# A decoder block's feed-forward part: four of seven products summed in one PSUM bank, memory pools laid anew at both layer changes, the last pair's norm moved into layer one

## The chip, the core and the metric

The kernel runs on one core of one Trainium2 chip. Its engines run side by side, each through its own instructions in a fixed order: PE (TensorE, matrix products), DVE (VectorE), ACT (ScalarE), POOL (GpSimd) and SP, which here issues nearly all DMAs. An engine waits for the others by semaphores, and nothing behind a waiting instruction runs before it. The metric is the time of one execution on the device in microseconds, as the median of several runs.

## The reference, cut to what matters

One decoder block over 2048 tokens of width 1024; the mixers in front are not touched by the change.

```python
h = h + jnp.einsum('bse,ed->bsd', mixed, w_out)
hn2 = rmsnorm(h, norm2_g)
up = jnp.einsum('bsd,df->bsf', hn2, w_up)        # 1024 -> 4096
act = jnp.square(jax.nn.relu(up))
h = h + jnp.einsum('bsf,fd->bsd', act, w_down)   # 4096 -> 1024
return rmsnorm(h, final_g)
```

## The kernel before

The tokens are handled in four tiles j of T = 512 columns, with the features on the 128 partitions. Every float32 operand is split into a high and a low part (`split`: ACT copies the high part, DVE subtracts it for the low one), and each 128x128 by 128x512 product is three matmuls.

**Output projection** (`tail`): for j = 0 to 3, eight chunks c, each of 24 matmuls into a bank `pd`. `add_acc` adds the result on DVE to the residual `acc`, and SP stores the sum to `hs[j][c]`. `norm2(j)` takes the root of the mean square (`pm` and `pr` are short matmuls on PE, the root itself runs on POOL) and multiplies `acc` by gain and root on DVE (L741).

**The two feed-forward layers** use a Strassen-Winograd scheme: the tiles are paired as (0, 1) and (3, 2), each matrix is halved both ways, and seven products of sums of quarters, P1 to P7, stand for eight. `PAIRS[0]` has its sums made by `sums_first`, which stores seven left operands to `su[0]`. For the second pair POOL stores the normed quarters to `su[1]` and `h21` (L745); `sums_second` loads them in layer one, in columns m = 4 to 7 of the first pair, makes four sums and stores them.

**Layer one** (`up`) runs over two pairs q, 16 columns m of the weights and the seven products s in a table `order`. One product is twelve matmuls (L907). `make_left` loads a left operand in two pieces into `sr` (two buffers) and splits them to `sa`; `make_weights` makes `hw` four products ahead; `make_left` runs `LA = 3` products ahead. Banks X, Y and Z have one buffer each: X holds P1 and then P2 on top, Y holds P6, P7 and P4 in a row, Z holds P5 and P3. After each product `post` takes from the banks what is complete so far: P1 is copied by ACT (L846), `u2`, `u3` and `a21` are made by DVE as Y plus that copy (L849, L855, L863), relu and square run on ACT (L840, L841), and results go to `sd` in DRAM (L837).

**Layer two** (`down`) loads 512 KB pieces of those results (`ar`, L965) and of the weights (`wr`, L929), splits them to `ad` and `wd`, and runs its seven products in steps of 48 matmuls (L1144) over the eight banks `pb`, two steps made ahead (`DA = 2`). The loads of the first two steps are on ACT's queue (`queue`), all later ones on SP's.

**What sets the order.** The program is written in order, and a scheduler then places each engine's instructions by its own estimate of times. Memory pools are laid out like a stack on two sides; a pool that takes the place of another waits for the last use of what lay there. `begin_ffn` opens layer one's pools at chunk c = 5 of the last tile's projection, prepares two left operands and the first weights, and the rest (`more`) is opened when the projection's pools are closed. The layer change in front of layer two lays `down`'s pools over those of `up`.

Of the kernel before, what the change touches and what calls it, by code (L numbers as in the profile page):

```python
# [15 lines left out]
P = 128  # L16
S = 2048
D = 1024
# [9 lines left out]
TB = T // P  # L28
WINDOWS = (2, 4, 8, 16)
# [4 lines left out]
RATIO_TAIL = 0.6  # L34
UA = 4
LA = 3
# [6 lines left out]
def hymba_block(ctx: ExitStack, tc: tile.TileContext, xT, gains, w_in, pool_w, w_out, w_up, w_down, out):  # L43
# [7 lines left out]
    wp = hp = pa = bigp = x0p = ntp = tmp = att = psd = psx = psz = pst = pso = olp = accp = acc2p = acc3p = None  # L51

    def open_pools(scope):
        nonlocal hp, wp, tmp, ntp, psd, psx, psz, pst, pso
        fpool = lambda name, bufs, **kw: scope.enter_context(tc.tile_pool(name=name, bufs=bufs, **kw))
        hp = fpool("hp", 2 * KD, side="right")
        ntp = fpool("ntp", 3, side="right")
        tmp = fpool("tmp", 2, side="right")
        wp = fpool("wp", 2, side="right")
        psz = fpool("psz", 2, space=PS)  # L60
        pso = fpool("pso", 1, space=PS)
        psd = fpool("psd", 2, space=PS)
        psx = fpool("psx", 1, space=PS)
        pst = fpool("pst", 2, space=PS)

    def open_big(scope):
        nonlocal bigp
        bigp = scope.enter_context(tc.tile_pool(name="bigp", bufs=1))
# [45 lines left out]
    zeros = const.tile([1, 1], I32, name="zeros")  # L114
    carry = const.tile([P, len(WINDOWS), PAD], F32, name="carry")
# [11 lines left out]
    h21 = [dram.tile([P, 2, T], F32, name=f"h21_{c}") for c in range(2)]  # L127
# [129 lines left out]
    def make_h():  # L257
        return hp.tile([P, 2, T], F32R, tag="h", name="h", align_bytes=256)
# [48 lines left out]
    def norm1_first():  # L307

        x, h = st[0]["x"], []
        for k in range(KD):  # L310
            d = make_h()
# [17 lines left out]
    def norm1(j):  # L329
        st[j]["h"] = normed(KD, lambda k: st[j]["x"][:, k], g1, make_h, lambda: st[j]["r"])  # L330
# [157 lines left out]
    def load_mix(j, n):  # L488
        st[j]["m"] = []
        for k in range(n):  # L490
            d = make_h()
# [8 lines left out]
    def tail(first):  # L500

        def root(j):

            if not (first and j < 2):
                drained(j)
                st[j]["todo"] = attn_norm(j, make_h)
# [18 lines left out]
        for j in range(NT):  # L525
# [3 lines left out]
            for c in range(KD):  # L529
# [10 lines left out]
                if c == 5 and j == NT - 1:  # L540
# [3 lines left out]

        def root_last():
            catch_up(len(later))
            norm2(NT - 1)
            catch_up(1)
        note(root_last)
# [174 lines left out]
    def square_of(j, key, c, first):  # L724
        if first:
            st[j][key] = tmp.tile([P, T], F32, tag="ss", name="ss", bufs=2)
# [9 lines left out]
    def norm2(j):  # L736
        acc = [st[j]["acc"][:, k] for k in range(KD)]
        later.append(lambda: st[j].update(rh=inv_rms(st[j]["sh"], D)))

        def put(k):  # L740
            nc.vector.scalar_tensor_tensor(acc[k], acc[k], g2[:, k:k + 1], st[j]["rh"], op0=ALU.mult, op1=ALU.mult)  # L741
# [34 lines left out]
    def up(pools, more):  # L776
# [3 lines left out]
        slots = [(q, m, s) for q in range(2) for m in range(NM) for s in range(7)]  # L780
# [17 lines left out]
        def make_weights(g):  # L798
            q, m, s = slots[g]
            which, i = order[s][1]  # L800
# [4 lines left out]
        def make_left(q, s):  # L805
            i, parts = order[s][0], []
            for c in range(2):
                r = srp.tile([P, 2, T], F32, tag="sr", name="sr")
                nc.sync.dma_start(r, su[q][i][c])
                t = saps[s].tile([P, 2, 2, T], F32R, tag="sa", name="sa", align_bytes=256)  # L810
# [4 lines left out]
        def sums_second(n):  # L815
            c, k = n // 2, n % 2
            new = lambda name: avp.tile([P, T], F32, tag="av", name=name)
            a11, a21, a12, s1 = new("ha11"), new("ha21"), new("ha12"), new("hs1")
            for t, of in ((a11, su[1][A11]), (a21, h21), (a12, su[1][A12]), (s1, su[1][A22])):
                nc.sync.dma_start(t, of[c][:, k])  # L820
            add = lambda to, x, y, op: nc.vector.tensor_tensor(to, x, y, op)
            add(s1, a21, s1, ALU.add)
            nc.sync.dma_start(su[1][S1][c][:, k], s1)
            add(a21, a11, a21, ALU.subtract)
            nc.sync.dma_start(su[1][S3][c][:, k], a21)
            add(a11, s1, a11, ALU.subtract)
            nc.sync.dma_start(su[1][S2][c][:, k], a11)
            add(a12, a12, a11, ALU.subtract)
            nc.sync.dma_start(su[1][S4][c][:, k], a12)

        def post(q, m, s):
# [12 lines left out]
            if s == 0:  # L844
                k["p1"] = pup.tile([P, T], F32, tag="p1", name="p1")
                nc.scalar.activation(k["p1"], x, AF.Copy)  # L846
            elif s == 1:
                k["u2"] = pup.tile([P, T], F32, tag="u2", name="u2")
                nc.vector.tensor_tensor(k["u2"], y, k["p1"], ALU.add)  # L849
            elif s == 2:  # L850
                act_of(A11, x, new("a11"))
                put(A11, k[A11])
            elif s == 3:
                k["u3"] = pup.tile([P, T], F32, tag="u3", name="u3")
                nc.vector.tensor_tensor(k["u3"], y, k["p1"], ALU.add)  # L855
            elif s == 4:
# [3 lines left out]
                put(A22, k[A22])  # L860
            elif s == 5:
                t = new("a21")
                nc.vector.tensor_tensor(t, y, k["p1"], ALU.add)  # L863
                act_of("A21", t, t)
# [8 lines left out]
            else:  # L873
# [10 lines left out]
        make_left(0, 0)  # L884
        add_weights(0, 0)
        for g in range(1, UA):
            make_weights(g)
        make_left(0, 1)
# [3 lines left out]
        for s in range(2, LA):  # L892
            make_left(0, s)
        for g, (q, m, s) in enumerate(slots):
            if g + LA < len(slots) and slots[g + LA][1] == 0:
                make_left(slots[g + LA][0], slots[g + LA][2])
            if q == 0 and s == 3 and 4 <= m < 8:
                sums_second(m - 4)
            bank, first = order[s][2:]
# [3 lines left out]
            last = (bank, s) in (("X", 2), ("Y", 5), ("Z", 6))  # L903
# [5 lines left out]
            post(q, m, s)  # L909
            if g + UA < len(slots):  # L910
                q2, m2, s2 = slots[g + UA]
                if s2 == 0:
                    add_weights(q2, m2)
                    n = q2 * NM + m2 + 1
                    if n < 2 * NM:
                        load(n // NM, n % NM)
                make_weights(g + UA)

    def down(pools):
# [18 lines left out]
        def make(g):  # L938
# [17 lines left out]
            else:  # L956
                w = blk(b22 if n == "P3" else b21, kk)
            t = t8.tile([P, 2, 2, T], F32R, tag="wd", name="wd", align_bytes=256)
            split((t[:, 0], t[:, 1]), w)
            if extra is not None:  # L960
                minus(blk(b12, kk), extra, 1, kk)
            left_ = {}
            for q in qs_:
                r = rs.tile([P, 2, T], F32, tag="ar", name="ar")
                queue[0].dma_start(r, sd[q][i][kk])  # L965
                left_[q] = s8.tile([P, 2, 2, T], F32R, tag="ad", name="ad", align_bytes=256)
                split((left_[q][:, 0], left_[q][:, 1]), r)
# [3 lines left out]
        ps = {}  # L971

# [347 lines left out]
```

## Time and profile before

| | before |
|---|---|
| median of 3 runs | 2015.91 us (2015.74 to 2019.39) |
| profiled execution | 2016.52 us, span 2014.6 us |
| mean granted TensorE clock | 0.983 |
| projection's last large matmul | starts at 722.85 us |
| layer one, second pair, undisturbed | 1100 to 1350 us |
| layer two's first matmul | starts at 1381.01 us |

Read the page's busy times first: PE is busy nearly all of the span. Such an engine is the bound, and what matters is where it falls behind its own pace; the other engines matter only where PE waits for them. For that one needs the table of stretches (busy time, count of instructions and granted clock in each), and then the timeline of the stretches that stand out. A busy PE can also be a slow PE, so the counts and the clock are read beside the busy time.

### The profile page before, as it was taken

To read this page: it belongs to the slowest core of one execution; us is meant where nothing else is said; L and a number is where in the kernel's file an instruction comes from. 1 tells how busy PE (TensorE), PEld (TensorE's weight loads), DVE (VectorE), ACT (ScalarE), POOL (GpSimd) and SP (SyncE) were. 2 spreads that over 40 slices of the span, in tenths; PEclk is the share of its full clock that TensorE was granted. 3 is DMA by queue.
4 is the path that set the end of the run, shared out by engine and by line. 5 is a ranking of instruction groups with operands and counts; after the bars stand their busy time and mean duration, and the time that the engine had idled before them with its cause. 6 is when DMAs were issued, how large, how long until landed. Compare 5 with 4: busy or idle time off the path is not lost.

```text
span 2014.6 us, 25952 instructions
## 1 busy us (share of the span) xinstructions
PE 1938.4 (96%) x9130; PEld 1613.1 (80%) x9130; DVE 1332.7 (66%) x1977; ACT 924.0 (46%) x1456; POOL 206.6 (10%) x415
## 2 busy tenths in 40 slices
PE   8999999999999979999999999996999999999997
PEld 6788788878888858878887888875888888888887
DVE  6877879667876976676687666654445453438474
ACT  5555556454644434545465455443232232333343
POOL 0212212102211120000000000000001000204010
PEclk9999999999999999999999999998999999999999
DMA  7675686788787874664565444457776654546472
GB/s 215 211 245 178 189 278 203 243 295 257 268 329 267 302 246 155 222 238 159 167 203 205 133 160 163 135 180 268 277 272 210 221 195 158 195 140 218 147 261 86
DMA packets 164396, 427.83 MB, mean 212 GB/s; under 512 B 19744, under 2 KB 25888, under 8 KB 160160
## 3 DMA queue, kind: packets, MB, share of 16 engines
q1 hardware_dynamic: 161824, 417.69, 61.9%
q10 hardware_dynamic: 1152, 4.19, 0.6%
q0 software_dynamic: 1280, 4.20, 0.6%
q8 instruction: 74, 1.21, 0.2%
q14 instruction: 66, 0.54, 0.1%
HBM read 284.44 MB, written 141.56 MB: 211 GB/s over the span
## 4 chain that ended last, share of the span: by engine, by line
PE 82%; DMA 7%; DVE 6%; issue 2%; ACT 1%; SPq 1%; POOL 0%; ACTq 0%; DVEq 0%; POOLq 0%
PE pb L1144 30%; PE pY L907 10%; PE pd L163 7%; PE pd L165 7%; PE pd L164 7%; PE pX L907 7%; PE pZ L907 7%; PE po L632 2%; DMA sr<-su 1%; PE pta L625 1%; DMA sd<-s 1%; DMA hs<-su 1%; DMA xt<-in_xT_dram 1%; PE pm L190 1%; PE pr L216 1%
## 5 line engine op out<-in xcount | busy, mean ns | idle before, releaser
L1144 PE MATMUL pb<-ad,wd 128*128 128x512 f32 x2640 | 603.1, 391 | 16.4 <-ACT ad L135 16.4
L1144 PEld LDWEIGHTS pb<-ad,wd 128*128 128x128 f32 x2640 | 496.3, 188 | 119.8 <-ACT ad L135 16.9
L163 PE MATMUL pd<-h,hl 128*128 128x512 f32 x768 | 309.6, 403 | 9.4 <-ACT h L312 6.3
L165 PE MATMUL pd<-h,hl 128*128 128x512 f32 x768 | 305.4, 398 | 0.9 <-DVE hl L136 0.9
L164 PE MATMUL pd<-h,hl 128*128 128x512 f32 x768 | 305.5, 398 | 0.3 <-DVE h L313 0.3
L907 PE MATMUL pY<-sa,hw 128*128 128x512 f32 x1152 | 281.2, 393 | 11.7 <-DVE sa L136 6.0
L907 PEld LDWEIGHTS pY<-sa,hw 128*128 128x128 f32 x1152 | 217.4, 189 | 59.9 <-DVE sa L136 7.1
L907 PE MATMUL pZ<-sa,hw 128*128 128x512 f32 x768 | 188.3, 393 | 8.0 <-DVE a L858 5.1
L907 PE MATMUL pX<-sa,hw 128*128 128x512 f32 x768 | 189.6, 390 | 1.9 <-ACT a L840 1.4
L135 ACT ACTIVATE ad<-ar 128x1024 fp32r<-128x1024 f32 x112 | 117.9, 1053 | 152.8 <-PE pb L1144 131.1
L136 DVE TENSOR_TENSOR ad<-ar,ad 128x1024 fp32r<-128x1024 f32 x112 | 141.9, 1268 | 65.5 <-ACT ad L135 65.5
L136 DVE TENSOR_TENSOR wd<-wr,wd 128x1024 fp32r<-128x1024 f32 x64 | 80.5, 1258 | 156.4 <-ACT wd L135 156.2
L163 PEld LDWEIGHTS pd<-h,hl 128*128 128x128 f32 x768 | 147.0, 191 | 38.8 <-ACT h L312 7.1
L907 PEld LDWEIGHTS pZ<-sa,hw 128*128 128x128 f32 x768 | 144.3, 189 | 41.3 <-ACT a L840 5.5
L165 PEld LDWEIGHTS pd<-h,hl 128*128 128x128 f32 x768 | 146.4, 191 | 30.3 <-DVE hl L136 1.4
L907 PEld LDWEIGHTS pX<-sa,hw 128*128 128x128 f32 x768 | 144.5, 188 | 32.6 <-ACT a L840 1.8
L164 PEld LDWEIGHTS pd<-h,hl 128*128 128x128 f32 x768 | 146.6, 191 | 28.7 <-DVE h L313 1.3
L135 ACT ACTIVATE wd<-wr 128x1024 fp32r<-128x1024 f32 x64 | 67.8, 1060 | 218.4 <-PE pb L1144 208.8
L135 ACT ACTIVATE hl<-raw 128x512 fp32r<-128x512 f32 x168 | 104.0, 629 | 124.5 <-PE pd L165 85.5
L136 DVE TENSOR_TENSOR hl<-raw,hl 128x512 fp32r<-128x512 f32 x168 | 114.8, 688 | 46.7 <-ACT hl L135 43.7
L135 ACT ACTIVATE hw<-rt 128x512 fp32r<-128x512 f32 x128 | 80.0, 626 | 91.3 <-PE pY L907 84.2
L840 ACT ACTIVATE a<-a 128x512 f32<-128x512 f32 x96 | 60.6, 632 | 128.7 <-DVE a L875 80.3
(186 smaller groups left out, 2343.0 us busy)
## 6 DMA issues: line engine op xcount, KB each, us to landing
ar<-sd SPq DMA_DIRECT2D x108, 512.0 KB, 4.4
wr<-in_w_down_dram SPq DMA_DIRECT2D x68, 512.0 KB, 3.8
rb<-in_w_up_dram SPq DMA_DIRECT2D x32, 1024.0 KB, 6.3
sd<-a SPq DMA_DIRECT2D x128, 256.0 KB, 4.6
raw<-in_w_in_dram SPq DMA_DIRECT2D x50, 512.0 KB, 4.3
sd<-s SPq DMA_DIRECT2D x96, 256.0 KB, 4.3
raw<-in_w_out_dram SPq DMA_DIRECT2D x32, 512.0 KB, 4.9
sr<-su SPq DMA_DIRECT2D x28, 512.0 KB, 4.1
```

The costliest lines, as they stand in the source:

```text
L135: nc.scalar.activation(hi, src, AF.Copy)
L136: return nc.vector.tensor_tensor(lo, src, hi.bitcast(F32), ALU.subtract)
L163: nc.tensor.matmul(ps, hl[:, 0, c], hi, start=(k == 0), stop=False)
L164: nc.tensor.matmul(ps, hl[:, 0, c], lo, start=False, stop=False)
L165: mm = nc.tensor.matmul(ps, hl[:, 1, c], hi, start=False, stop=(k == n - 1))
L190: marks["pm"] = nc.tensor.matmul(pm[:, c:c + 1], ss[:, c * P:(c + 1) * P], inv[n], start=(i == 0), stop=(i == len(parts) - 1))
L216: mm = nc.tensor.matmul(pr[:, b * P:(b + 1) * P], yr[:, x, b:b + 1].to_broadcast([P, P]), identr, start=(b == 0 and x == 0), stop=(b == TB ...
L625: nc.tensor.transpose(pt[:, x * P:(x + 1) * P], sg[:, x * P:(x + 1) * P], ident)
L632: nc.tensor.matmul(po[:, p * 256 + to:p * 256 + to + hi - lo], vw[:, 2 * p + v], at[:, x, lo:hi], start=(p == 0 and n == 0 and x == 0), sk ...
L840: nc.scalar.activation(t, src, AF.Relu)
L907: nc.tensor.matmul(t, w[:, wx, c], a[:, ax, c % 2], start=first and c == 0 and x == 0, stop=last and c == G - 1 and x == 2, skip_group_che ...
L1144: nc.tensor.matmul(ps[q, n], t[:, wx, c, n * P:(n + 1) * P], left_[q][:, ax, c], start=(kk == 0 and c == 0 and x == 0), stop=(kk == 7 and ...
```

## The change

- **Banks in layer one.** P1, P6, P7 and P4 all add up in Y, P2 alone is in X, P5 and P3 in Z. So P1, `u2` and `u3` are now plain copies of Y by ACT between the products, and DVE makes one sum with the copy of P1, for P2. X, Y, Z and a new R have two buffers each. The next column's P1 stands before this column's P4 and P3.
- **Layer two** sums P1, P6, P7 and P4 in one bank in the same way, and P5 with P3; the DVE sums between them become ACT copies or go.
- **The last pair's norm** goes out of the projection. `hs` in DRAM keeps the tiles before the norm; the root of tile 2 is kept in `rlast`, the root of tile 3 is made within layer one (behind its second and ninth product), and `sums_second` multiplies by gain and root when it loads a quarter, in columns 4, 6, 8 and 10, in three parts. It stores the quarters and the sums by SP; POOL's stores and `h21` go.
- **Left operands.** `begin_ffn` stands at c = 3 and prepares four left operands (`LB`); `sr` has four buffers (`SR`), and `LA` is 5.
- **Pools.** Half of the projection's operands lie on the left side, which `begin_ffn` frees; the DMA scratch area is smaller; `down`'s pools are laid in another order: `ar` (pool `rs`), `wr` (`rt`) and `wd` (`t8`) now lie on the pools of layer one's first weights, loads and left operands, where they lay in part on the tiles of its results (`avp`). All of layer two's loads are on SP's queue, with `ar` ahead of the split of the weights.

The core of the diff:

```diff
+SR = 4
+LB = 4
 UA = 4
-LA = 3
+LA = 5
...
-        hp = fpool("hp", 2 * KD, side="right")
+        hpb = fpool("hpb", KD, side="right")
...
+        hpa = scope.enter_context(tc.tile_pool(name="hpa", bufs=KD))
...
-                if c == 5 and j == NT - 1:
+                if c == 3 and j == NT - 1:
                     note(begin_ffn)
...
-        later.append(lambda: st[j].update(rh=inv_rms(st[j]["sh"], D)))
+        later.append(lambda: st[j].update(rh=inv_rms(st[j]["sh"], D, rlast[:, 0] if j == 2 else None)))
...
-            a = j == PAIRS[1][0]
-            if j in PAIRS[1]:
-                to = su[1][A12 if a else A22] if k >= 4 else su[1][A11] if a else h21
-                nc.gpsimd.dma_start(to[k % 4 // 2][:, k % 2], acc[k])
-        later.extend(lambda k=k: put(k) for k in range(KD))
+        if j in PAIRS[0]:
+            later.extend(lambda k=k: put(k) for k in range(KD))
...
-        order = ((A11, (0, 0), "X", True), (S2, (1, 1), "Y", True), (A12, (0, 1), "X", False), (S3, (1, 2), "Y", False),
-                 (S1, (1, 0), "Z", True), (A22, (1, 3), "Y", False), (S4, (0, 2), "Z", False))
+        what = {"P1": (A11, (0, 0), "Y", True, False), "P2": (A12, (0, 1), "X", True, True),
+                "P6": (S2, (1, 1), "Y", False, False), "P5": (S1, (1, 0), "Z", True, False),
+                "P7": (S3, (1, 2), "Y", False, False), "P4": (A22, (1, 3), "Y", False, True),
+                "P3": (S4, (0, 2), "Z", False, True)}
+        order = list(what)
+
+        slots = [cols[0] + ("P1",)]
+        for n, c in enumerate(cols):
+            slots += [c + (s,) for s in ("P2", "P6", "P5", "P7")]
+            slots += [c2 + ("P1",) for c2 in cols[n + 1:n + 2]]
+            slots += [c + (s,) for s in ("P4", "P3")]
...
+            def normed_of(h, i):
+                t, j = new("hn"), PAIRS[1][h]
+                nc.sync.dma_start(t, hs[j][i])
+                nc.vector.scalar_tensor_tensor(t, t, g2[:, i:i + 1], rlast[:, j - 2], op0=ALU.mult, op1=ALU.mult)
+                return t
...
+            def copy(name):
+                k[name] = pup.tile([P, T], F32, tag=name, name=name)
+                nc.scalar.activation(k[name], y, AF.Copy)
...
+            if g == 1:
+                y = inv_root(mean_squares([sslast], D, psu, "R"), nc.gpsimd)
...
+            elif g == 8:
+                pr = psu.tile([P, T], F32, tag="R", name="pr")
+                spread(pr, yrlast)
+                nc.scalar.activation(rlast[:, 1], pr, AF.Copy)
...
-        made, queue = {}, [nc.scalar]
+        made = {}
...
-            queue[0].dma_start(t, w_down[i, kk] if isinstance(i, int) else td[int(i[1]) - 1][kk])
+            nc.sync.dma_start(t, w_down[i, kk] if isinstance(i, int) else td[int(i[1]) - 1][kk])
...
-            if n_ == "P1":
-                nc.scalar.activation(val("p1", q)[:, n], b, AF.Copy)
-            elif n_ == "P6":
-                add(val("u2", q), val("p1", q))
-                add_residual(val("p1", q)[:, n], j0, 0, n)
-            elif n_ == "P7":
-                add(val("u3", q), val("u2", q))
-            elif n_ == "P4":
-                add(val("c21", q), val("u3", q))
-                add_residual(val("c21", q)[:, n], j1, 0, n)
+            if n_ in CHAIN:
+                nc.scalar.activation(val(CHAIN[n_], q)[:, n], b, AF.Copy)
+                if n_ in ("P1", "P4"):
+                    add_residual(val(CHAIN[n_], q)[:, n], j0 if n_ == "P1" else j1, 0, n)
...
-            rsp, tmp2, rlp = spool("rsp", 2), spool("tmp2", 2), spool("rlp", 2)
-            t8, rt, rs, s8 = spool("t8", DA + 1), spool("rt", 4), spool("rs", 3), spool("s8", 2 * DA + 1)
+            rlp, tmp2, rs, rt, t8 = spool("rlp", 2), spool("tmp2", 2), spool("rs", 3), spool("rt", 4), spool("t8", DA + 1)
+            s8, pup, rsp = spool("s8", 2 * DA + 1), spool("pup", 8), spool("rsp", 2)
```

How the order of the instructions moves is shown at three places. The first is DVE at the change from the projection to layer one, before: `acc_7414` is the last tile, `sa` are split left operands, `hw` weights.

```order
L136 TENSOR_TENSOR sa_8130<-sr_8128,sa_8130 128x1024
L136 TENSOR_TENSOR hw_8259<-rb_8083,hw_8259 128x512
L741 SCALAR_TENSOR_TENSOR acc_7414<-acc_7414,gains_130,r_8028 128x512 x8
L136 TENSOR_TENSOR sa_8153<-sr_8151,sa_8153 128x1024
L136 TENSOR_TENSOR hw_8282<-rt_8204,hw_8282 128x512
L136 TENSOR_TENSOR sa_8158<-sr_8156,sa_8158 128x1024
```

And of the change, where the last projection sum is followed by the sixth and fifth of the fresh operands (P4 and P7):

```order
L731 TENSOR_TENSOR acc_7418<-pd_7979,acc_7418 128x512
L142 TENSOR_TENSOR sa_8072<-sr_8070,sa_8072 128x1024
L142 TENSOR_TENSOR sa_8077<-sr_8075,sa_8077 128x1024
L180 TENSOR_TENSOR sslast_144<-sslast_144,sq_8006 128x512
L142 TENSOR_TENSOR hw_8120<-rb_8040,hw_8120 128x512
L142 TENSOR_TENSOR hw_8147<-rt_7800,hw_8147 128x512
L798 TENSOR_TENSOR rt_8187<-rb_8040 128x512
L800 TENSOR_TENSOR rt_8187<-rb_8040 128x512
L142 TENSOR_TENSOR sa_8044<-sr_8042,sa_8044 128x1024
```

The eight multiplications of the norm are gone from between the operands' splits. The second place is PE in an undisturbed column of layer one, before: the number behind a bank's letter is the column's buffer, so the rows show P5, P7, the next column's P1, P4 and P3.

```order
L907 MATMUL pZ_10228<-sa_8125,hw_10164 128x512 x6
L907 MATMUL pZ_10228<-sa_8130,hw_10164 128x512 x6
L907 MATMUL pY_10167<-sa_8097,hw_10146 128x512 x6
L907 MATMUL pY_10167<-sa_8102,hw_10146 128x512 x6
L907 MATMUL pX_10299<-sa_7865,hw_10225 128x512 x6
L907 MATMUL pX_10299<-sa_7870,hw_10225 128x512 x6
L907 MATMUL pY_10167<-sa_8153,hw_10182 128x512 x6
L907 MATMUL pY_10167<-sa_8158,hw_10182 128x512 x6
```

And of the change, from the next column's P1 over P7 and the next column's P2 to P4:

```order
L934 MATMUL pY_10259<-sa_7787,hw_10194 128x512 x4
L934 MATMUL pY_10109<-sa_8044,hw_10173 128x512 x6
L934 MATMUL pY_10109<-sa_8049,hw_10173 128x512 x6
L934 MATMUL pY_10259<-sa_7787,hw_10194 128x512 x2
L934 MATMUL pX_10326<-sa_7792,hw_10256 128x512 x6
L934 MATMUL pX_10326<-sa_7797,hw_10256 128x512 x6
L934 MATMUL pY_10109<-sa_8072,hw_10211 128x512 x6
L934 MATMUL pY_10109<-sa_8077,hw_10211 128x512 x6
```

Between P7 and P4, which share a bank and have a copy between them, stand fourteen matmuls of other banks. The third place is the change to layer two, before on ACT: relu and square of the last column (L840, L841), then the first loads and splits of layer two.

```order
L841 ACTIVATE a21_13016<-a21_13016 128x512
L840 ACTIVATE a12_13040<-a12_13040 128x512
L841 ACTIVATE a12_13040<-a12_13040 128x512
L965 DMA ar_13099<-sd0_0_0_308 128x1024
L965 DMA ar_13104<-sd1_0_0_364 128x1024
L965 DMA ar_13118<-sd0_0_1_309 128x1024
L135 ACTIVATE ad_13101<-ar_13099 128x1024
```

And of the change on SP, where `sd1_6_6` and `sd1_0_7` are stores of the last but one and of the last column:

```order
L993 DMA ar_13101<-sd0_0_0_312 128x1024
L993 DMA ar_13102<-sd1_0_0_368 128x1024
L993 DMA ar_13120<-sd0_0_1_313 128x1024
L864 DMA sd1_1_6_382<-a12_12785 128x512
L864 DMA sd1_6_6_422<-s4_12790 128x512
L864 DMA sd1_0_7_375<-a11_12809 128x512
L962 DMA wr_13099<-in_w_down_dram 128x1024
L962 DMA wr_13114<-in_w_down_dram 128x1024
```

The loads stood behind the last square of the last column on ACT and now stand ahead of the last column's stores on SP. On ACT of the change the first `ad` split stands behind three relus and three squares that follow the copy of P7, and the fourth load (`ar_13121`, the second pair's of the second step) is on SP behind most of the last stores. In the last column P7 and P4 follow each other on PE with nothing between them.

More of the change, by code (lines that the diff above doesn't have):

```diff
@@ L799, in make_weights @@
             q, m, s = slots[g]
-            which, i = order[s][1]
+            which, i = what[s][1]
+            if s == "P2":
+                add_weights(q, m)
             hl = hlp.tile([P, 2, G, P], F32R, tag="hw", name="hw", align_bytes=256)
@@ L805, in make_left @@
         def make_left(q, s):
-            i, parts = order[s][0], []
+            i, parts = what[s][0], []
             for c in range(2):
@@ L813, in make_left, with sums_second @@
             left_ops[q, s] = parts
[L815 removed]
+        SUMS, second = ("P2", "P5", "P4"), {}
+        def sums_second(n, part):
             c, k = n // 2, n % 2
             new = lambda name: avp.tile([P, T], F32, tag="av", name=name)
[L818 to L820 removed]
+            keep = lambda i, t: nc.sync.dma_start(su[1][i][c][:, k], t)
             add = lambda to, x, y, op: nc.vector.tensor_tensor(to, x, y, op)
[L822 to L829, printed above, removed]
+            def normed_of(h, i):
[3 more added lines that the diff above has]
+                return t
+            if part == 0:
+                second["a21"], a22 = normed_of(1, n), normed_of(1, 4 + n)
+                second["s1"] = new("hs1")
+                add(second["s1"], second["a21"], a22, ALU.add)
+                keep(A22, a22)
+                keep(S1, second["s1"])
+            elif part == 1:
+                a11, a21, s1 = normed_of(0, n), second["a21"], second["s1"]
+                add(a21, a11, a21, ALU.subtract)
+                second["s2"] = new("hs2")
+                add(second["s2"], s1, a11, ALU.subtract)
+                keep(A11, a11)
+                keep(S3, a21)
+                keep(S2, second["s2"])
+            else:
+                a12, s4 = normed_of(0, 4 + n), new("hs4")
+                keep(A12, a12)
+                add(s4, a12, second["s2"], ALU.subtract)
+                keep(S4, s4)
         def post(q, m, s):
@@ L842, in act_of @@
                 k[i] = t
[L844 to L856, printed above, removed]
+            def copy(name):
+                k[name] = pup.tile([P, T], F32, tag=name, name=name)
+                nc.scalar.activation(k[name], y, AF.Copy)
+            if s == "P1":
+                copy("p1")
+            elif s == "P2":
+                t = new("a11")
+                nc.vector.tensor_tensor(t, x, k["p1"], ALU.add)
+                act_of(A11, t, t)
+                put(A11, t)
+            elif s == "P6":
+                copy("u2")
+            elif s == "P7":
+                copy("u3")
                 t = new("a22")
@@ L883, in up @@
         make_weights(0)
-        make_left(0, 0)
-        add_weights(0, 0)
+        make_left(0, "P1")
+        make_left(0, "P2")
         for g in range(1, UA):
             make_weights(g)
-        make_left(0, 1)
+        for s in order[2:LB]:
+            make_left(0, s)
         yield
@@ L891, in up @@
         load(0, 1)
-        for s in range(2, LA):
-            make_left(0, s)
+        lefts = [(g, q, s) for g, (q, m, s) in enumerate(slots) if m == 0 and not (q == 0 and s in order[:LB])]
         for g, (q, m, s) in enumerate(slots):
[L895 to L899, printed above, removed]
+            while lefts and lefts[0][0] <= g + LA:
+                make_left(*lefts.pop(0)[1:])
+            if q == 0 and 4 <= m < 12 and m % 2 == 0 and s in SUMS:
+                sums_second(m // 2 - 2, SUMS.index(s))
+            bank, first, last = what[s][2:]
             if first:
```

95 lines of the change are left out of this document (46 added, 49 removed).

## The prediction

> **What bounds the kernel now.** First the page's busy times, then the table of stretches, to see where the bounding engine does not run at its pace.
>
> ```profile
> PE 1938.4 (96%) x9130; PEld 1613.1 (80%) x9130; DVE 1332.7 (66%) x1977; ACT 924.0 (46%) x1456; POOL 206.6 (10%) x415
> ```
>
> TensorE (PE) is busy 96% of the span. The change removes no large product, so it can only win what PE loses by standing still or by running at a lower clock. Where that is, the stretches tell (length, then busy time and count of each engine, granted clock, DMA share, GB/s):
>
> ```profile
> 1100.00:1350.00 250.00, 250.00 (x1105) 207.11 (x1104) 165.40 (x261) 125.13 (x209) 0.00 (x0) 1.00 0.45 150
> 720.00:760.00 40.00, 26.67 (x100) 19.80 (x99) 27.11 (x36) 17.86 (x24) 10.72 (x23) 0.83 0.67 231
> 840.00:910.00 70.00, 67.82 (x296) 55.00 (x295) 53.76 (x87) 33.73 (x58) 0.00 (x0) 1.00 0.71 244
> 1050.00:1090.00 40.00, 35.46 (x149) 26.93 (x148) 33.29 (x48) 25.32 (x38) 0.00 (x0) 1.00 0.65 228
> 1350.00:1400.00 50.00, 30.76 (x127) 24.52 (x126) 23.61 (x24) 16.82 (x20) 0.00 (x0) 0.83 0.83 282
> 1400.00:1900.00 500.00, 500.00 (x2207) 414.06 (x2206) 245.02 (x223) 153.98 (x163) 52.13 (x32) 1.00 0.61 205
> ```
>
> 1100 to 1350 is layer one undisturbed: 1105 matmuls in 250 us, 0.2262 us each, so a product of twelve takes 2.72 us. Four stretches fall behind that pace. The first holds 16 short matmuls of the norm beside the large ones:
>
> ```profile
> 728.52 0.95 PE L190 MATMUL pm<-inv,ss 128*128 128x1 f32 x8
> 737.27 1.27 PE L216 MATMUL pr<-identr,yr 128*128 128x128 f32 x8 [1.27 <-POOL yr L226]
> ```
>
> What each stretch loses, waits and slow clock together, is its length less its matmuls times 0.2262:
> - 720 to 760, the change from the output projection to layer one. Less the 16 short ones, some 2 us, it holds 84: 40 - 84 x 0.2262 - 2 = **19.0 us**.
> - 840 to 910, the columns in which the second pair's sums are made: 70 - 296 x 0.2262 = **3.0 us**.
> - 1050 to 1090, the change from the first pair to the second inside layer one: 40 - 149 x 0.2262 = **6.3 us**.
> - 1350 to 1400, the change to layer two: 50 - 127 x 0.2262 = **21.3 us**.
>
> Together 49.6 us. The other losses lie before 690 us, and there the two programs stand in the same order on every engine. Who ends PE's waits (total, times, longest):
>
> ```profile
> PE pb L1144 <- ACT ad L135: 16.4, 1, 16.4
> PE pY L907 <- DVE sa L136: 6.0, 2, 5.1
> PE pZ L907 <- DVE a L858: 5.1, 1, 5.1
> PE pZ L907 <- DVE a L875: 2.1, 3, 1.0
> ```
>
> **Change to layer two.** The timeline there (start, length, engine or queue, what; in brackets the idle time before it and who ended it):
>
> ```profile
> 1357.97 0.68 DVE L855 TENSOR_TENSOR u<-pY,p 128x512 f32<-128x512 f32 x1
> 1358.80 2.98 PE L907 MATMUL pY<-sa,hw 128*128 128x512 f32 x12 [2.81 <-DVE u L855]
> 1361.62 2.96 PE L907 MATMUL pZ<-sa,hw 128*128 128x512 f32 x12
> 1367.60 0.38 SPq L837 DMA_DIRECT2D sd<-s  x1
> 1373.36 5.11 ACTq L965 DMA_DIRECT2D ar<-sd  x3
> 1379.90 1.06 ACT L135 ACTIVATE ad<-ar 128x1024 fp32r<-128x1024 f32 x1 [8.99 <-DMA ar<-sd]
> 1380.99 1.23 DVE L136 TENSOR_TENSOR ad<-ar,ad 128x1024 fp32r<-128x1024 f32 x1 [9.35 <-ACT ad L135]
> 1381.01 19.37 PE L1144 MATMUL pb<-ad,wd 128*128 128x512 f32 x76 [16.43 <-ACT ad L135]
> ...
> 1367.60 5.73 DMA sd<-s
> 1373.36 6.44 DMA ar<-sd
> ```
>
> The last two lines are of the chain that ended last. The first `ar` load is issued at 1373.36, when a store of layer one's result (1367.60 + 5.73) has landed: the buffer of `ar` lies on memory of the tiles that are stored. The data is there 6.5 us later, and then comes a split. The relaid pools put `ar` and `wr` on memory that layer one has finished with, and the order has the three first `ar` loads ahead of the last column's stores. The loads of the first two steps also move from ScalarE's queue to SP's, where a row that waits holds up all behind it. With the memory free, the 16.43 us go. What is late next is worked out from the order. PE now runs P7 and P4 of the last column on one bank with nothing between them, and P4 waits for a ScalarE copy:
>
> ```profile
> L846 ACT ACTIVATE p<-pX 128x512 f32<-128x512 f32 x32 | 19.0, 594 | 6.3 <-PE pX L907 3.9
> L849 DVE TENSOR_TENSOR u<-pY,p 128x512 f32<-128x512 f32 x32 | 22.1, 690 | 22.9 <-PE pY L907 22.9
> L840 ACT ACTIVATE a<-a 128x512 f32<-128x512 f32 x96 | 60.6, 632 | 128.7 <-DVE a L875 80.3 <-DVE a L858 37.8 <-DVE a L863 8.4
> L841 ACT ACTIVATE a<-a 128x512 f32<-128x512 f32 x128 | 80.4, 629 | 3.1 <-ACT a L840 0.3
> ```
>
> That copy takes 0.59 us and its hand-overs some 0.2, my estimate: 0.8 us. From its end ScalarE has three relus and three squares and then the first `ad` split, 6 x 0.63 + 1.06 = 4.8 us, two of them behind VectorE sums of 0.69 us: 6.2 us, against 5.44 us of PE (P4 and P3). With hand-overs I take 1.5 us. The low half of that split stands behind four VectorE sums, of which PE covers some: 1.0 us. Sum **3.3 us**. The ends are 0 (ScalarE keeps up) and 8.8 us (a load and both halves of a split in full: 6.5 + 1.06 + 1.23).
>
> **Change to layer one.**
>
> ```profile
> 725.13 30.25 SPq L809 DMA_DIRECT2D sr<-su  x9
> 740.50 5.38 DVE L741 SCALAR_TENSOR_TENSOR acc<-acc,gains,r 128x512 f32<-128x512 f32 x8
> 745.80 1.22 DVE L136 TENSOR_TENSOR sa<-sr,sa 128x1024 fp32r<-128x1024 f32 x1
> 747.07 4.17 PE L907 MATMUL pY<-sa,hw 128*128 128x512 f32 x11 [5.05 <-DVE sa L136]
> 752.71 1.06 ACT L135 ACTIVATE sa<-sr 128x1024 fp32r<-128x1024 f32 x1 [8.28 <-DMA sr<-su]
> 756.38 3.33 PE L907 MATMUL pZ<-sa,hw 128*128 128x512 f32 x7 [5.13 <-DVE a L858]
> ...
> sr<-su SPq DMA_DIRECT2D x28, 512.0 KB, 4.1
> ```
>
> Here PE waits for left operands, each a pair of loads and splits. One of them stands behind the eight products of the last pair's norm (740.50, 5.38 us). The next ones wait for loads that only two `sr` buffers pass on: a load and its split take 4.1 + 1.06 + 1.23 = 6.4 us, where PE uses an operand up in 2.72. After the change the norm is gone from this place, four operands (10.9 us of PE) are ready instead of two (5.4), and four buffers keep two operands in flight. A fresh operand takes 4.1 + 2 x 1.06 + 1.23 = 7.5 us, which 10.9 covers and 5.4 did not. I leave **1.0 us** for hand-overs; the ends are 0 and one uncovered round of 6.4 us.
>
> The norm's sixteen products of that pair come back inside layer one, four of them and the four sums of before in every second of eight columns, with four loads and seven stores in place of four and four. VectorE is busy 53.76 of 70 us there now. It loses two sums per column to ScalarE, and Z gets a second bank, so the waits of `pZ` on L875 lose their cause: 3.0 us go, and 3.0 is also the upper end of what may stay.
>
> **Change of pairs.** The same two `sr` buffers hold this one up:
>
> ```profile
> 1065.70 6.24 SPq L809 DMA_DIRECT2D sr<-su  x2
> 1069.28 1.06 ACT L135 ACTIVATE sa<-sr 128x1024 fp32r<-128x1024 f32 x1 [3.43 <-DMA sr<-su]
> 1070.39 0.50 PE L907 MATMUL pY<-sa,hw 128*128 128x512 f32 x1 [1.58 <-ACT sa L135]
> ```
>
> With four, and operands asked for five products ahead instead of three (13.6 us against 8.2, where 7.5 are needed), I leave **0.5 us**; the ends are 0 and 6.3.
>
> **One bank for four products** costs nothing in the steady columns by my reading, and gains nothing, since PE is already busy 250 of 250 us. The tightest place is P7 to P4: fourteen matmuls lie between, 3.17 us, to cover 0.8. Two sums (L849, L855) become copies. In layer two (500 of 500 us busy) seven groups of six matmuls, 9.5 us, lie between a product and the next on its bank. Uncovered, a copy would cost 0.8 us a column, 51 us over 64 columns. The POOL DMAs that go were off PE's path.
>
> **The sum.** The profiled execution took 2016.5 us (span 2014.6 and 1.9 around it). 2016.5 - 49.6 = 1966.9 without these losses; + 3.3 + 1.0 + 0.5 = 1971.7, say **1972 us**. The median of the runs, 2015.9, is 0.6 lower.
>
> **A rule on the clock.** After the 16.43 us wait, 76 matmuls take 19.37 us, 0.253 from one start to the next, which is 2.0 us over the pace, and the granted clock of that stretch is 0.83; between 1050 and 1090 there are waits like the 1.58 us above, and the clock stays at 1.00. The Trainium skill, page "TensorE: Matmul & The Clock Gate", section "Part 1: The HAM clock gate (the "warmup" mystery)", puts the drop to half rate after one idle window of about 3.4 us; the trace agrees as far as it goes. By it none of the waits I leave would cost clock. The same page's section "A second HAM failure mode: psum-queue depth-cycling" speaks against this change: short idles between groups that cycle through banks would make the clock swing, and by it the waits that I leave would each bring slow matmuls. The stretch from 1050 to 1090 speaks against that.
>
> **The rivals.**
> - *Layer two's wait stays in part* (20%). The second pair's `ar` for the second step is still loaded behind the last stores. For it: a store took 5.7 us to land. Against: it is due only after 72 matmuls of layer two, 16.3 us. It gives 8.8 in place of 3.3, and 2.0 of slow clock: 1979.
> - *Layer one's early loads hold up the projection* (10%). They begin two products earlier, where the DMA engines were already full:
>
> ```profile
> 670.00:690.00 20.00, 20.00 (x90) 16.54 (x89) 18.00 (x25) 7.55 (x14) 0.00 (x0) 1.00 1.00 375
> ```
>
>   Four more loads of 0.52 MB at 375 GB/s are 5.6 us of transfer. If the weights wait for all of it: 1972 + 5.6 = 1978.
> - *Clock* (5%). The short waits bring a slow stretch at both layer changes, 2.0 us each: 1976.
> - *Slower than before* (3%). ScalarE comes late to the copies of the shared bank because relu, square and splits stand ahead of them in its order. The gain of 44 us is used up when each of 64 columns loses 0.7 us, that is, when P7's copy ends 3.9 us after P7 instead of 0.8; relu, square and one split ahead are only 1.9. At 0.8 us a column: 1972 + 51 = 2023.
> - *The change doesn't do what it says* (2%). The buffers still meet live memory, and the wait at layer two stays whole: 1972 - 3.3 + 21.3 = 1990.
>
> My forecast has 60%. The range reaches from 1966, all losses gone, to 1987, where the first three rivals meet (5.5 + 2.0 + 5.6 and 2.0 over the forecast). Faster by over 0.2% (about what a measurement of this kernel can tell from no change) 0.95, within it 0.02, slower 0.03.
>
> **What would show it.** Right: between 1300 and 1350 of the new span PE waits less than 5 us and the clock stays at 1.00; 40 us around the first `pY` hold about 170 matmuls; no `pZ` wait on a VectorE sum in the columns with the second pair's sums; `ar` loads issued before the last column's stores. Wrong: a repeated wait of `pY` on a ScalarE copy in each column, or `pd` waiting for `raw` loads.

## The result, and the profile after

The changed kernel takes 1969.59 us (median of 4 runs, 1966.36 to 1973.38) against 2016.11 us before; the ratio is 0.9766, with a 95% interval of 0.9745 to 0.9788. The profiled execution took 1970.99 us, 45.5 less than the profiled one of before; the forecast was 1972.

The page of after, its busy times, and then the table of stretches (length, busy time and count of each engine, granted clock, DMA share, GB/s):

```profile
PE 1929.2 (98%) x9130; PEld 1610.7 (82%) x9130; DVE 1268.3 (64%) x1881; ACT 958.7 (49%) x1544; POOL 191.9 (10%) x399
```
```profile
690.00:780.00 90.00, 90.00 (x411) 74.74 (x411) 62.94 (x93) 53.36 (x84) 13.72 (x30) 1.00 0.59 202
840.00:910.00 70.00, 70.00 (x310) 57.96 (x310) 53.24 (x86) 36.65 (x66) 0.00 (x0) 1.00 0.71 239
1000.00:1100.00 100.00, 98.08 (x426) 80.69 (x425) 71.75 (x105) 64.08 (x105) 0.00 (x0) 0.98 0.59 201
1300.00:1350.00 50.00, 48.66 (x212) 39.19 (x211) 32.71 (x43) 28.27 (x43) 0.00 (x0) 1.00 0.86 314
1300.00:1400.00 100.00, 98.66 (x433) 80.57 (x432) 58.18 (x64) 43.20 (x57) 0.00 (x0) 1.00 0.82 291
```

The same account as in the prediction, length less matmuls times 0.2262: the change to layer one, inside 690 to 780, loses nothing any more (TensorE busy 90 of 90); neither do the columns with the second pair's sums (70 of 70). The change of pairs, inside 1000 to 1100, still loses 100 - 426 x 0.2262 = 3.6 us, and the change to layer two, inside 1300 to 1400, 2.1 us. Of 49.6 us some 44 are gone. TensorE's waits between 650 and 1450 (total, times, longest) are two lines:

```profile
PE pY L934 <- ACT u L873: 2.6, 2, 1.9
PE pb L1171 <- DVE ad L142: 0.6, 1, 0.6
```

Both waits of the first line are for ScalarE's copy of the bank that is shared: one in the last column of the first pair, one in the last column of all. The timelines there, first of TensorE and ScalarE at the change of pairs, then of SyncE, TensorE and ScalarE at layer two (start, length, engine, what; in brackets the idle time before and who ended it):

```profile
1023.65 2.88 PE L934 MATMUL pX<-sa,hw 128*128 128x512 f32 x12
1028.45 4.45 PE L934 MATMUL pY<-sa,hw 128*128 128x512 f32 x12 [1.92 <-ACT u L873]
...
1020.59 0.62 ACT L868 ACTIVATE a<-a 128x512 f32<-128x512 f32 x1
1026.86 1.06 ACT L141 ACTIVATE sa<-sr 128x1024 fp32r<-128x1024 f32 x1 [5.64 <-DMA sr<-su]
1027.82 0.58 ACT L873 ACTIVATE u<-pY 128x512 f32<-128x512 f32 x1
```
```profile
1306.39 1.28 SPq L993 DMA_DIRECT2D ar<-sd  x3
...
1326.71 2.88 PE L934 MATMUL pY<-sa,hw 128*128 128x512 f32 x12
1330.28 3.01 PE L934 MATMUL pY<-sa,hw 128*128 128x512 f32 x12 [0.69 <-ACT u L873]
1333.13 2.88 PE L934 MATMUL pZ<-sa,hw 128*128 128x512 f32 x12
1336.03 2.20 PE L1171 MATMUL pb<-ad,wd 128*128 128x512 f32 x8
1338.86 21.38 PE L1171 MATMUL pb<-ad,wd 128*128 128x512 f32 x93 [0.64 <-DVE ad L142]
...
1329.63 0.60 ACT L873 ACTIVATE u<-pY 128x512 f32<-128x512 f32 x1 [2.04 <-PE pY L934]
1334.93 2.94 ACT L141 ACTIVATE ad<-ar 128x1024 fp32r<-128x1024 f32 x3
```

At the change of pairs P7 of the old column is through by 1023.65, and its copy would take 0.6 us. But in ScalarE's queue a split of the new pair's `sa` stands ahead of it, and that split waits 5.64 us for its `sr` load. So the copy comes at 1027.82, and P4, which adds to the same bank, starts 2.1 us late. At layer two the `ar` loads now go out at 1306.39, before the last column's stores, and the 16.43 us wait is gone. The signs that the prediction named hold: between 1300 and 1350 TensorE waits 1.3 us in all, the clock stays at 1.00, and no `pZ` wait is in the list.

### The profile page after: what moved, and what is told of

It reads as the page before. It is cut to its first block, busy times and chain, and to the rows that moved or that the text cites. A ratio compares the mean times of both kernels' runs of the same rounds, so it can differ in the third digit from the quotient of the medians.

```text
span 1969.2 us, 25982 instructions
## 1 busy us (share of the span) xinstructions
PE 1929.2 (98%) x9130; PEld 1610.7 (82%) x9130; DVE 1268.3 (64%) x1881; ACT 958.7 (49%) x1544; POOL 191.9 (10%) x399
## 4 chain that ended last, share of the span: by engine, by line
PE 91%; DMA 3%; DVE 3%; ACT 1%; issue 1%; SPq 0%; POOL 0%; DVEq 0%; ACTq 0%; POOLq 0%
PE pb L1171 30%; PE pY L934 17%; PE pZ L934 8%; PE pd L169 8%; PE pd L171 8%; PE pd L170 8%; PE pX L934 4%; PE po L632 2%; PE pta L625 1%; PE pr L222 1%; PE pm L196 1%; PE pz L567 1%; PE pz L568 1%; DMA xt<-in_xT_dram 1%; PE pb L1134 1%
## 5 line engine op out<-in xcount | busy, mean ns | idle before, releaser
L934 PE MATMUL pY<-sa,hw 128*128 128x512 f32 x1536 | 366.1, 390 | 2.6 <-ACT u L873 2.6
L934 PEld LDWEIGHTS pY<-sa,hw 128*128 128x128 f32 x1536 | 288.9, 188 | 63.6 <-ACT u L873 3.4
L142 DVE TENSOR_TENSOR hw<-rt,hw 128x512 fp32r<-128x512 f32 x128 | 87.6, 686 | 77.1 <-ACT hw L141 77.0
L873 ACT ACTIVATE u<-pY 128x512 f32<-128x512 f32 x64 | 38.1, 595 | 119.6 <-PE pY L934 119.5
L934 PE MATMUL pX<-sa,hw 128*128 128x512 f32 x384 | 92.7, 389 | 0.0
L966 DVE TENSOR_TENSOR wr<-wr 128x1024 f32<-128x1024 f32 x32 | 40.0, 1251 | 76.2 <-DMA wr<-in_w_down_dram 76.2
```

What stands on the lines that cost most here:

```text
L142: return nc.vector.tensor_tensor(lo, src, hi.bitcast(F32), ALU.subtract)
L873: nc.scalar.activation(k[name], y, AF.Copy)
L934: nc.tensor.matmul(t, w[:, wx, c], a[:, ax, c % 2], start=first and c == 0 and x == 0, stop=last and c == G - 1 and x == 2, skip_group_che ...
L966: nc.vector.tensor_tensor(b, a, b, ALU.subtract)
```

## The experiments

The runs of one group shared a chip and the runs of before beside them. Ratios are to before, with 95% intervals; the changed kernel's is 0.9766.

### The norm of the last pair put back (e1)

```diff
+            if j in PAIRS[1]:
+                to = su[1][A12 if a else A22] if k >= 4 else su[1][A11] if a else h21
+                nc.gpsimd.dma_start(to[k % 4 // 2][:, k % 2], acc[k])
+        later.extend(lambda k=k: put(k) for k in range(KD))
...
-            if q == 0 and 4 <= m < 12 and m % 2 == 0 and s in SUMS:
-                sums_second(m // 2 - 2, SUMS.index(s))
+            if q == 0 and s == "P7" and 4 <= m < 8:
+                sums_second(m - 4)
```

> The changed kernel with one part undone: the last pair's norm and its stores stand between the output projection and layer one again, and the sums of the second pair are made from the stored result in four columns. Theory (the eight products of the norm on VectorE and the root ahead of them, queued ahead of the splits of layer one's operands, were most of the 19.0 us that TensorE lost there): TensorE loses 10 to 16 us between 690 and 760, time 1980 to 1986. Rival (the loads through two buffers were most of it, and they are four now): at most 4 us lost there, time 1970 to 1974.

Measured: 1984.89 us, ratio 0.9835 [0.9811, 0.9860]. Its stretch, and who ends TensorE's longest waits:

```profile
690.00:780.00 90.00, 79.95 (x330) 64.03 (x330) 63.34 (x90) 42.77 (x66) 20.37 (x46) 0.92 0.67 236
```
```profile
PE pm L197 <- DVE sslast L181: 3.7, 1, 3.7
PE pd L170 <- DVE acc L738: 2.4, 1, 2.4
PE pY L925 <- ACT p L864: 2.0, 1, 2.0
```

81 matmuls fewer than in the changed kernel: 18.3 us, above what the theory expected, and almost as much as the 19.0 that stood there before, with four load buffers and four operands in place. So with the norm at this place the loss is there, and buffers alone don't cure it. But the way is not the one that the theory named: none of TensorE's waits here is for a left operand `sa`. The norm's short products `pm` wait 3.7 us for the last sum of squares, the projection waits 2.4 us for a sum that VectorE makes behind the other tile's eight multiplications, and 1.9 us go to weights `hw` (two shorter waits). The waits are 10.1 us in all (90 less 79.95); the rest is slow clock, 0.92 in this stretch. (The time rose by 15.3 and not 18.3; this kernel loses nothing at the change of pairs, where the changed one loses 3.6.)

### Two load buffers (e2, e11), and three products ahead (e12)

```diff
-SR = 4
+SR = 2
```

> The changed kernel with two buffers for the raw left operands of layer one in place of four. Theory (two buffers pass on one operand at a time, 6.4 us for each where TensorE uses one up in 2.72): a wait for sa splits comes back at the change of pairs, about 1 to 6 us, and 0 to 6 at the change to layer one; time 1972 to 1980. Rival (four operands made ahead and five asked ahead suffice by themselves): 1968 to 1971.

> The changed kernel with two load buffers, beside the changed kernel on one chip. Theory (two buffers hold the splits back in ScalarE's queue, so that fewer of them stand ahead of the copy): 2 to 4 us less than the changed kernel, no wait of TensorE at the change of pairs. Rival (the earlier run was lower by chance): within 1 us of it.

The third of them also has

```diff
-LA = 5
+LA = 3
```

> The changed kernel with two load buffers and operands asked three products ahead instead of five, as before the change, but with the four premade operands and the new order of the products. Theory (buffers and lead made the 6.3 us at the change of pairs): TensorE waits there for sa splits again, 2 to 6 us. Rival (the old order of the products and its two banks made them): under 1 us lost there.

Measured: e2 1967.33 us, ratio 0.9751 [0.9732, 0.9770]; the same kernel again, e11, 1968.63, 0.9761 [0.9741, 0.9781], beside the changed kernel (e9) with 1970.17, 0.9754 [0.9733, 0.9775]; e12 1966.97 (two runs). None is told from the changed kernel by its time. The stretch with the change of pairs, of e2, e11 and e12 in turn:

```profile
1000.00:1100.00 100.00, 100.00 (x443) 82.81 (x442) 72.70 (x106) 65.79 (x108) 0.00 (x0) 1.00 0.66 224
```
```profile
1000.00:1100.00 100.00, 98.10 (x430) 80.34 (x429) 71.77 (x104) 64.31 (x105) 0.00 (x0) 1.00 0.63 214
```
```profile
1000.00:1100.00 100.00, 100.00 (x443) 82.82 (x442) 76.60 (x113) 66.86 (x109) 0.00 (x0) 1.00 0.64 216
```

The theory of e2 and e12 fell: with two buffers, and even with two buffers and three products ahead, nothing is lost there in one execution each. In another execution of the two-buffer kernel (e11) 2.7 us were, with waits for `sa` splits of 1.0 and 0.9 us: it runs close to the edge. In time e11 lies 1.5 us under e9, between what its theory and its rival said, and the intervals overlap. With the rest of the change in place, then, neither the buffers nor the lead are needed to be rid of most of the 6.3 us. That the new order of products and banks took them away is not shown: it wasn't tried by itself, and the moved norm and the four premade operands were also in place.

### Two operands made ahead (e3)

```diff
-LB = 4
+LB = 2
...
-LA = 5
+LA = 3
...
+            sap[2], sap[3] = (spool(f"sap{s}", 2) for s in (2, 3))
```

> The changed kernel with two left operands made before layer one in place of four, asked three products ahead in place of five; four load buffers stay. Theory (two ready operands are 5.4 us of products, a fresh one takes 7.5 us): one uncovered round, 2 to 6 us at the change to layer one; time 1972 to 1976. Rival (with the norm gone from there and four buffers, nothing waits): 1968 to 1971.

Measured: 1979.42 us, ratio 0.9815 [0.9791, 0.9839].

```profile
690.00:780.00 90.00, 86.73 (x391) 71.12 (x390) 60.65 (x88) 50.59 (x80) 16.58 (x30) 1.00 0.54 191
...
1300.00:1400.00 100.00, 93.85 (x398) 76.26 (x397) 52.63 (x59) 40.63 (x55) 0.00 (x0) 0.95 0.76 266
```

At the change to layer one 20 matmuls are missing, 4.5 us, within the size that the theory expected. (The three products ahead alone don't do it: e12 has those, and is busy 89.5 of the 90 us.) But the round of fresh operands that the theory named is not what TensorE waits for. Its waits between 690 and 780 are these four:

```profile
PE pY L934 <- ACT u L873: 1.1, 1, 1.1
PE pr L222 <- POOL yrlast L939: 1.1, 1, 1.1
PE pr L222 <- POOL yr L232: 0.8, 1, 0.8
PE pr L222 <- POOL yrlast L940: 0.3, 1, 0.3
```

None is for an `sa`. One is for a copy of the shared bank, which starts on ScalarE directly behind an `sa` split; the other three are for the norm's roots, which POOL makes. So with the norm moved, two ready operands cost time here, but a fresh operand that takes 7.5 us is not shown to be why. The other large loss is at the change to layer two, 10.0 us. The two pools that are opened later also move layer two's buffers, and that these now meet live memory may be the reason, but it is not shown: the first `ar` load goes out at 1306.4 as in the changed kernel, and TensorE still waits 3.8 and 1.6 us for `ad`. The time, 3 us above what was expected, says nothing of the operands.

### The pools of before (e4), the queue of before (e5), both (e6)

```diff
-            sap[6], pup, rbb, avp = spool("sap6", 2), spool("pup", 2), spool("rbb", 1), spool("avp", 11)
+            avp, rbb, pup, sap[6] = spool("avp", 11), spool("rbb", 1), spool("pup", 2), spool("sap6", 2)
...
-            rlp, tmp2, rs, rt, t8 = spool("rlp", 2), spool("tmp2", 2), spool("rs", 3), spool("rt", 4), spool("t8", DA + 1)
+            rsp, tmp2, rlp = spool("rsp", 2), spool("tmp2", 2), spool("rlp", 2)
+            t8, rt, rs, s8 = spool("t8", DA + 1), spool("rt", 4), spool("rs", 3), spool("s8", 2 * DA + 1)
```

> The changed kernel with the pools of both layers laid in the order of before; loads on the sync engine's queue and ahead of the last stores as now. Theory (the buffers of ar on memory of tiles that layer one still stores set the wait at layer two): the first ar load is issued only after a store has landed, TensorE waits 9 to 17 us at its first pb products; time 1978 to 1988. Rival (the queue and the place of the loads in it set the wait, not the memory): under 3 us more than the changed kernel, 1969 to 1973.

```diff
-        made = {}
+        made, queue = {}, [nc.scalar]
...
-            rows = {q: rs.tile([P, 2, T], F32, tag="ar", name="ar") for q in qs_}
-            for q in qs_:
-                nc.sync.dma_start(rows[q], sd[q][i][kk])
...
+                r = rs.tile([P, 2, T], F32, tag="ar", name="ar")
+                queue[0].dma_start(r, sd[q][i][kk])
```

> The changed kernel with the loads of layer two's first two steps on ScalarE's queue and each ar load behind its step's weights, as before; the pools as now. Theory (the memory set 9 of the some 19 us between the two kernels at layer two; the queue and the place of the loads set the rest): the ar loads are issued later than 1306 and TensorE loses 5 to 12 us at the change, time 1973 to 1980. Rival (with free memory the queue does not matter): at most 3.5 us lost there, 1968 to 1972.

> The changed kernel with both the pools and the queue and load order of before; the banks and the order of the seven products stay. Theory (memory and queue together are the whole of it): TensorE loses 17 to 22 us at layer two, time 1984 to 1990. Rival (the old order of the products, its last sum on VectorE, had its own part in the wait): 10 to 14 us lost, 1977 to 1982.

Measured: e4 1979.15 us, 0.9810 [0.9781, 0.9840]; in the next group, where before took 2019.93, e5 1971.94, 0.9756 [0.9739, 0.9772], and e6 1982.10, 0.9796 [0.9774, 0.9819]. The stretch of layer two's change in e4, e5 and e6:

```profile
1300.00:1400.00 100.00, 91.77 (x389) 74.59 (x389) 50.30 (x56) 40.02 (x52) 0.00 (x0) 0.95 0.76 270
```
```profile
1300.00:1400.00 100.00, 97.88 (x431) 80.39 (x430) 56.78 (x63) 43.37 (x57) 0.00 (x0) 1.00 0.81 285
```
```profile
1300.00:1400.00 100.00, 90.39 (x382) 73.40 (x381) 52.81 (x59) 39.83 (x53) 0.00 (x0) 0.93 0.73 260
```

By the account above 12.0, 2.5 and 13.6 us are lost, against 2.1 in the changed kernel and 21.3 before, in one profiled execution each. By these, memory is worth 9.9 us (the interval of e4's time still touches that of the changed kernel, so the size rests on the stretch); the queue and the place of the loads are worth 0.4 when the memory is free, and 1.6 when it isn't. So the rival of e5 holds, and that of e6: 7.7 us of the old loss came from neither. What remains between e6 and before at this place is the rest of the change, the order of the products on the banks above all; it was not undone alone. In e4 the users of the tile `ar` show where the memory bites (what they waited for: total, times):

```profile
  DMA sd<-a: 4.8, 1
  DMA sd<-s: 4.6, 1
```

The first line is ScalarE's half of a split, the second VectorE's. Both wait for stores, not for the load, which went out at 1322.3, some 19 us before (the slowest `ar` load in this stretch took 7.8): so the buffers of the halves that they write, `ad`, lie on live memory as well. By this trace, freeing `ar` alone would not have been enough.

### P7 and P4 side by side in every column (e7)

```diff
+        slots = [c + (s,) for c in cols for s in ("P1", "P2", "P6", "P5", "P7", "P4", "P3")]
...
+                if s in ("P1", "P2") and fourth:
+                    behind.enter_context(tc.issue_after(fourth[0].ins))
```

> The changed kernel with the first product of the next column queued behind P4, so that P7 and P4 stand side by side on the shared bank in every column, as in the last one. Theory (the copy between them costs 0.85 us and the products between hide it): 0.85 us lost in each of 64 columns, 54 us, time 2022 to 2026. Rival (other products still stand between in the queue, or the copy is hidden another way): under 15 us more, below 1985.

Measured: 2019.96 us, ratio 0.9996 [0.9984, 1.0007]: the whole gain is gone. The waits between 690 and 1420, and one column's rows:

```profile
PE pY L934 <- ACT u L870: 35.5, 58, 1.8
```
```profile
1102.17 0.39 PE L934 MATMUL pZ<-sa,hw 128*128 128x512 f32 x1
1103.02 3.01 PE L934 MATMUL pY<-sa,hw 128*128 128x512 f32 x12 [0.46 <-ACT u L870]
1106.72 5.28 PE L934 MATMUL pY<-sa,hw 128*128 128x512 f32 x22 [0.69 <-ACT u L870]
```

The price of an uncovered copy is what the last column of the changed kernel showed (0.69 us of wait, and a start 0.85 us later than at the usual pace). The sum in the expectation came near for a wrong reason: there are 32 columns, not 64 (384 matmuls on `pX`, twelve a column), and in each two copies are uncovered, since a single matmul stands between P6 and P7 too: 46 us in 32 columns are 1.4 a column. Without the products between, then, the shared bank costs as much as the whole change gains.

### One bank for Z (e8)

```diff
-                ps[q, m, bank] = psu.tile([P, T], F32, tag=bank, name="p" + bank)
+                ps[q, m, bank] = psu.tile([P, T], F32, tag=bank, name="p" + bank, bufs=1 if bank == "Z" else 2)
```

> The changed kernel with one bank for Z in place of two. Theory (the second bank took the waits of pZ on VectorE's sums away): waits of pZ on a VectorE sum come back in the columns with the second pair's sums, 3 to 8 us in all, time 1972 to 1978. Rival (VectorE's lighter columns alone took them away): no such wait, 1968 to 1971.

Measured: 1972.03 us, ratio 0.9763 [0.9745, 0.9782], not told from the changed kernel. One wait of `pZ` on a VectorE sum is there between 690 and 1000, 0.5 us. The theory's 3 to 8 us are not: the second bank was not what took away most of these waits. (At layer two it loses 5.9 us in its one profiled execution, 416 matmuls between 1300 and 1400; why was not followed up.)

### The copy ahead of the split (e10), beside the changed kernel (e9)

```diff
-                make_left(*lefts.pop(0)[1:])
+                loaded.append(lefts.pop(0))
+                load_left(*loaded[-1][1:])
...
+            while loaded and loaded[0][0] <= g + LS:
+                with tc.issue_after(copied[0].ins):
+                    split_left(*loaded.pop(0)[1:])
```

> The changed kernel itself, as the measure for the three runs beside it on this chip. Both theories: the wait of pY on ScalarE's copy at the change of pairs, 1.9 us, and the slow matmuls behind it are there again; ratio to before 0.975 to 0.979.

> The changed kernel with layer one's raw left operands of the second pair loaded as now, but each one's splits on ScalarE queued behind the copy of the product before, so that the copy of P7 in the last column of the first pair no longer stands behind a split that waits for its load. Theory (the place in ScalarE's queue makes the wait): the 1.9 us wait and its slow matmuls go, 3 to 4 us less than the changed kernel beside it. Rival (the loads themselves are late, the wait moves to the split operands): no gain, or a wait of pY or pX on sa in its place.

Measured: e9 1970.17 us (1961.82 to 1972.56), e10 1965.36 (1963.16 to 1970.07), ratio 0.9747 [0.9731, 0.9763]. The first 690 us and the stretch with the change of pairs, of e9 and of e10:

```profile
0.00:690.00 690.00, 664.30 (x3452) 560.63 (x3453) 528.46 (x904) 369.60 (x662) 108.57 (x292) 0.98 0.74 248
1000.00:1100.00 100.00, 98.00 (x426) 80.61 (x425) 71.86 (x105) 64.00 (x104) 0.00 (x0) 0.98 0.58 198
```
```profile
0.00:690.00 690.00, 666.15 (x3475) 562.65 (x3476) 533.27 (x912) 372.88 (x667) 113.35 (x297) 0.99 0.75 250
1000.00:1100.00 100.00, 99.84 (x441) 82.37 (x440) 73.89 (x107) 66.10 (x110) 0.00 (x0) 1.00 0.61 204
```

The wait is there again in e9 (2.00 us) and gone in e10: 15 matmuls more in the same 100 us, 3.4 us. The traces show that in e9, as in the changed kernel, the copy stands behind a split that waits 5.7 us for its load. They don't show that the place alone made the difference. In e10 the longest wait of a split for its load in this stretch is 1.6 us, so the load was no longer late either. And in e8, which has the changed kernel's queue and four buffers, that wait was at most 1.0 us and only 0.5 us was lost. On these traces the loss is there where a late load and a split ahead of the copy meet; a late load with the copy in front was not measured. Whether e10 is faster as a whole the times don't settle: the intervals overlap, and the two profiled executions differ by 23 matmuls, 5.2 us, before layer one has begun. It is the lowest median of all the runs.

## Why the prediction came out right, step by step

- *The four losses, 49.6 us:* right in place and size; 5.7 of them stay, where 4.8 were forecast. The sum by the measured residuals is 1972.6, and 1971.0 was profiled; the first 690 us alone hold six matmuls more than before, 1.4 us. That the residuals agree so well is partly luck: 2.2 us too much at the two layer changes and 3.1 too little at the change of pairs nearly cancel.
- *Change to layer two, 3.3 left:* measured 2.1. P4's wait for the copy, 0.8, is 0.85; the low half of the split, 1.0, is 1.0. The step that failed is the first split, sized at 1.5: `pb` starts 0.2 us late, since ScalarE's six relus and squares follow each other every 0.59 us and the first of the three splits is through some 5.8 us after the copy (1334.93 + 1.06 less 1330.23), not 6.9.
- *"With the memory free, the 16.43 us go":* the outcome is right, the attribution too broad. Memory is 9.9 us (e4), the queue up to 1.6 (e6), and 7.7 belong to neither. What the step leaves out is the rest of the change, not undone alone.
- *Change to layer one, 1.0 left:* 0 measured. Moving the norm (e1) and making four operands ahead (e3) are each needed. The four load buffers, which the step counted with them, are not: with two TensorE is busy 89.7 (e2) and 90.0 (e11) of the 90 us. The step's route, TensorE waiting for fresh operands, didn't come back in e1 or e3: their waits there are for the norm's own sums and roots, for weights, and for copies.
- *Sums' columns, 0 left:* right; "Z gets a second bank" is not the reason (e8). VectorE's two sums less per column and the order of products remain as reasons, not tested.
- *Change of pairs, 0.5 left:* wrong, 3.6 measured, and by another mechanism than the one named. The wait for `sr` buffers is gone, but not because there are four (e2, e12). A copy of the shared bank behind a split that waits for its load took its place (the timeline of after, and e9). It doesn't come each time: other kernels with four buffers lose between 0 (e1) and 3.6 us (e5) there.
- *The rival "slower than before"* had that very mechanism, "ScalarE comes late to the copies". It decided in one column of 32. Its price was mis-sized: "64 columns" should read 32, so that 0.8 a column is 26 us, not 51, and the point of decision 1.4 us a column, not 0.7. The row of the copies in the prediction says x32. e7 shows that the side that was forecast slower is real.
- *"By it none of the waits I leave would cost clock":* did not hold; see the last section.

## What to carry to other kernels

A copy that frees an accumulator is only as cheap as what stands ahead of it in its engine's queue: look there for work that waits for a DMA, above all where a stage changes, and queue it behind the copy. When a wait is blamed on memory, undo memory, queue and order one at a time: here the layout was half of it, and the load buffers that looked like a cure could be left out. And when an experiment brings the expected loss back, look whom TensorE waits for: twice here the size was near and the wait was another.

## What the hardware showed unexpectedly

The slow clock came after waits far shorter than the 16.43 us one. The matmuls behind a wait at the change of pairs, in e5 and in e4:

```profile
1029.81 4.61 PE L934 MATMUL pY<-sa,hw 128*128 128x512 f32 x12 [1.84 <-ACT u L873]
```
```profile
1026.74 3.06 PE L934 MATMUL pY<-sa,hw 128*128 128x512 f32 x12 [1.88 <-ACT u L873]
```

After 1.84 us (e5) and 1.92 us (after, shown above) twelve matmuls take 4.61 and 4.45 us, at a granted clock of 0.57 and 0.65 over the four microseconds from their start: 1.4 to 1.6 us more than the 3.06 in e4. After 1.88 us (e4) and 1.56 us (e3) they run at full pace, and so they do after the 2.81 us wait before layer two in the kernel of before, 2.98 us for twelve. So no single length of wait divides the two here. The Trainium skill, page "TensorE: Matmul & The Clock Gate", section "Part 1: The HAM clock gate (the "warmup" mystery)", puts the drop after an idle window of about 3.4 us; the waits of 1.84 and 1.92 us that were followed by slow matmuls do not agree with that.

The other thing is how far two executions are apart before any of the changed work has begun: in the first 690 us TensorE got through 3439 matmuls in one profiled execution (e12) and 3475 in another (e10), 8.1 us apart, and 31 of these 36 lie in the first 300 us. Their spans, 1970.3 and 1962.2, differ by 8.1 as well. These are two kernels with one execution each, so that all the spread comes from there is not shown.
